# Rows for the feed-forward part: the second pair fetched with the first, and both transposed ahead of the last output projection

## The chip, the cores and the metric

The kernel runs on one core of a Trainium2 chip. It is written in Bass with the Tile framework, which allots buffers from pools, places the semaphore waits and orders each engine's instructions. The engines are TensorE (PE), VectorE (DVE), ScalarE (ACT), GpSimd (POOL) and SyncE (SP, which only issues transfers here). The metric is the device time of one execution in microseconds (us), the median of several runs.

## The reference, cut to what matters

A trunk of two layers over 1024 latent rows and 256 context rows of width 1024. Each layer mixes (attention and a state-space scan side by side, one input and one output projection) and then runs a SwiGLU feed-forward part. The change stands where the one goes over into the other:

```python
for l in range(DEPTH):                       # DEPTH = 2
    update_ctx = l < DEPTH - 1               # the last layer drops the context rows
    h_l = rmsnorm(x_lat, norm_mix_pre[l]) * (1.0 + sc1_l) + sh1_l
    h_c = rmsnorm(x_ctx, norm_mix_pre[l]) * (1.0 + sc1_c) + sh1_c
    m_l, m_c = hybrid_mixer(h_l, h_c, ..., w_out[l], update_ctx)
    x_lat = x_lat + g1_l * rmsnorm(m_l, norm_mix_post[l])

    f_l = rmsnorm(x_lat, norm_ffn_pre[l]) * (1.0 + sc2_l) + sh2_l
    x_lat = x_lat + g2_l * rmsnorm(swiglu(f_l, w_gate[l], w_up[l], w_down[l]), norm_ffn_post[l])
    if update_ctx:
        x_ctx = x_ctx + g1_c * rmsnorm(m_c, norm_mix_post[l])
        f_c = rmsnorm(x_ctx, norm_ffn_pre[l]) * (1.0 + sc2_c) + sh2_c
        x_ctx = x_ctx + g2_c * rmsnorm(swiglu(f_c, ...), norm_ffn_post[l])
```

## The kernel before, in words

**Tiles.** The 1280 rows are ten tiles of 128 rows: tiles 0 and 1 are the context, 2 to 9 the latent rows. Layer 1 takes only tiles 2 to 9 past its attention. Every product in f32 is made of three matmuls on parts: each operand is split into a high part and the rest, and `mm3` (L228 to L230) adds high by high, high by rest and rest by high.

**Weights.** They stream through the kernel in a planned sequence. A 512 KB piece is fetched by SP into one of two buffers `raw_t` (beside the context's feed-forward in layer 0 also into a spare `raw_u`); ACT casts the high part into a slot `w_t` (L114), and DVE or POOL subtracts it from the raw piece for the rest (L115). There are five slots; a slot is free once its matmuls are done, and a raw buffer once both steps have read it.

**Buffers.** `x()` gives one of six buffers `xt` (128 x 1024, a whole row tile), `s2()` one of eight buffers `s2t` (128 x 512). The matmuls write into five PSUM banks `ps_w` and three `ps_s`.

**Attention's end.** Attention works in units of a tile and a group of heads. When a tile's units are done, `oproj` projects it with w_out (L228 to L230, out of `att_wo` or `w_t` and the attention's output `xt` or `att_b`), `postnorm` normalises and gates the result (two DVE steps L832 and one L838) and writes the row tile to memory, where the feed-forward part finds it. The call `early(0)` comes just ahead of the last unit's values, then follows the second-last tile's projection, then `early(1)`, then the last tile's projection (which goes through the weight pieces one by one and frees their slots), then `early(2)`.

**Rows for the feed-forward part.** They are taken in pairs of tiles. `pre_load` fetches a pair into two `xt` buffers (L992), `row_halves` (L380) fetches a tile into two `s2t` buffers of half a row each. `pre_scale` squares and sums each row on ACT (L243, two steps a tile), makes the reciprocal root on POOL (L245, L235, L236) and scales the rows on POOL (L375, one step for a whole tile, two for halves). The flip (`flip_steps`) then makes columns of the pair: sixteen transposes on PE (L402) into four `ps_w` banks, eight scale-and-shift steps on ACT (L405) into four `s2t` buffers, four copies for the high part on POOL (L409) and four subtractions for the rest on DVE (L410), into `hc` (context) or `ha` (latent). With `keep`, the shifted columns also go out to memory (L412), to be combined later. For the pairs of tiles 6, 7 and 8, 9 there are `quads` instead, which transpose (L1016), shift (L1020) and combine the columns with those kept (L1026 to L1034 on DVE and POOL) into the blocks `h_hb`, `h_t3`, `h_t4` that the latent feed-forward multiplies.

**What runs where, before.** `early(0)` fetches and scales the first pair (tiles 0, 1 in layer 0; 2, 3 in layer 1) and, in layer 1, fetches tiles 6, 7 as halves. `early(1)` flips the first pair and fetches and scales the second (tiles 2, 3; in layer 1 tiles 4, 5, and it scales the halves of 6, 7). `early(2)` flips the second pair and in layer 0 fetches and scales the third (tiles 4, 5). After attention, layer 0 runs the context's gate and up projections (L228 to L230, `ps_w<-hc,w_t`), with `fill_c` between their pieces: its first step flips the third pair, later ones run the quads. Layer 1 goes straight to the latent feed-forward, which begins with the quads of tiles 6, 7.

Of the kernel before, what the change touches and what calls it, by code (L numbers as in the profile page):

```python
# [17 lines left out]
P = 128  # L18
# [36 lines left out]
class Trunk:  # L55
# [314 lines left out]
    def pre_scale(self, xs):  # L370
        for a in xs:
            whole = not isinstance(a, list)
            r = self.row_rstd([a[:, 0:512], a[:, 512:1024]] if whole else a, D)
            for b in [a] if whole else a:
                self.nc.gpsimd.tensor_scalar(b, b, r, 1.0, op0=ALU.mult, op1=ALU.mult)  # L375

    def row_halves(self, t, src):
        a = [self.s2(), self.s2()]
        for i in range(2):
            self.nc.sync.dma_start(a[i], self.x_src(src, t)[:, i * 512:(i + 1) * 512])  # L380
        return a
# [5 lines left out]
    def flip_steps(self, xs, span, i, l, which, keep=None):  # L387
        nc = self.nc
        ps = self.psw
        cc = self.cols[l, which]  # L390
        n = len(xs) * P
        nm, v, col0 = span[0], 1 if span[0] == "hc" else 0, 2 * i * P
        if i == 0:
            self.hT[nm] = self.hT_alloc(nm)
        dst = self.hT[nm]
        for k2 in range(0, KT, 2):
            t = ps()
            h = self.s2()
            for k in range(2):
                kt = k2 + k  # L400
                for j, a in enumerate(xs):
                    nc.tensor.transpose(t[:, k * n + j * P:k * n + (j + 1) * P], a[:, kt * P:(kt + 1) * P], self.ident)  # L402
            for k in range(2):
                kt = k2 + k
                nc.scalar.activation(h[:, k * n:(k + 1) * n], t[:, k * n:(k + 1) * n], AF.Identity,  # L405
                                     bias=cc[:, 8 * v + kt:8 * v + kt + 1], scale=cc[:, 16 + 8 * v + kt:17 + 8 * v + kt])
            hv = h[:, 0:2 * n].rearrange("p (k n) -> p k n", k=2)
            hi = dst[:, k2:k2 + 2, 0, col0:col0 + n]
            nc.gpsimd.tensor_scalar(hi, hv, 1.0, 1.0, op0=ALU.mult, op1=ALU.mult)  # L409
            nc.vector.tensor_tensor(dst[:, k2:k2 + 2, 1, col0:col0 + n], hv, hi.bitcast(F32), op=ALU.subtract)  # L410
            if keep:
                nc.scalar.dma_start(keep[k2 // 2, i], h)  # L412
            yield
# [587 lines left out]
    def quads(self, l, xs, i, B):  # L1001
        nc = self.nc
        cc = self.cols[l, 1]
        tt = nc.vector.tensor_tensor
        v = lambda a: a.rearrange("p (k n) -> p k n", k=2)
        for k2 in range(0, 4, 2):
            qa, qb = self.x(), self.x()
            for half in range(2):
                nc.sync.dma_start(qa[:, half * 512:(half + 1) * 512], self.hf_d[l][(k2 + 4 * half) // 2, i])
            for half in range(2):  # L1010
                t = self.psw()
                for k in range(2):
                    kt = k2 + 4 * half + k
                    for j, a in enumerate(xs):
                        rows = a[half][:, kt % 4 * P:(kt % 4 + 1) * P] if isinstance(a, list) else a[:, kt * P:(kt + 1) * P]
                        nc.tensor.transpose(t[:, k * 256 + j * P:k * 256 + (j + 1) * P], rows, self.ident)  # L1016
                for k in range(2):
                    kt = k2 + 4 * half + k
                    o = half * 512 + k * 256
                    nc.scalar.activation(qb[:, o:o + 256], t[:, k * 256:(k + 1) * 256], AF.Identity, bias=cc[:, kt:kt + 1], scale=cc[:, 16 + kt:17 + kt])  # L1020
            b11, b21, b12, b22 = qa[:, 0:512], qa[:, 512:1024], qb[:, 0:512], qb[:, 512:1024]

            def put(name, src, eng):
                d = B[name][:, k2:k2 + 2, :, 256 * i:256 * i + 256]
                nc.scalar.copy(d[:, :, 0], v(src))
                eng.tensor_tensor(d[:, :, 1], v(src), d[:, :, 0].bitcast(F32), op=ALU.subtract)  # L1026

            if l:
                put("B22", b22, nc.vector)
            else:  # L1030
                keep = self.s2()
                nc.gpsimd.tensor_scalar(keep, b22, 1.0, 1.0, op0=ALU.mult, op1=ALU.mult)
                nc.scalar.dma_start(self.b22_d[k2 // 2, i], keep)
            tt(b11, b12, b11, op=ALU.subtract)  # L1034
            tt(b12, b22, b12, op=ALU.subtract)
            tt(b22, b22, b11, op=ALU.subtract)
            put("T2", b22, nc.vector)
            put("T3", b12, nc.vector)
            put("T1", b11, nc.vector)
            tt(b21, b22, b21, op=ALU.subtract)  # L1040
            put("T4", b21, nc.gpsimd)
            yield
# [193 lines left out]
def emit(nc, tc, I, out, dump=None):  # L1236
    with ExitStack() as es:
        k = Trunk(nc, tc, es, I, out)
        k.hT, k.fgrow = {}, (None, None)
        k.plan()  # L1240
        SC, SA, SB = k.SPANS
# [15 lines left out]
        for l in range(DEPTH):  # L1257
# [3 lines left out]
            with tc.tile_pool(name=f"kv{l}", bufs=1, reuse_waits="tile") as kv:  # L1261
# [10 lines left out]
                fl = {}  # L1272

                def early(stage):
                    keep = k.hf_d[l]
                    if stage == 0:
                        cols()
                        fl[0] = k.pre_pair(SC if l == 0 else SA, 0, 2 * l, l, 1, keep if l else None)
                        if l:
                            fl[2] = [k.row_halves(t, 2) for t in (6, 7)]  # L1280
                    elif stage == 1:
                        fl[0]()
                        fl[1] = k.pre_pair(SA, l, 2 * l, l, 1, keep)
                        if l:
                            k.pre_scale(fl[2])
                    else:
                        fl[1]()
                        if l == 0:
                            fl[2] = k.pre_pair(SA, 1, 0, 0, 1, keep)

                gate, ss = k.ssd(l, kv)
                zf = itertools.chain([step(ss)] * (len(qt) - 1), [lambda: None])
# [3 lines left out]
                def zfill():  # L1296
                    i = next(nz)
                    if i == 2:
                        k.att_keys(l)
                    if i == len(qt) - 4:  # L1300
                        k.att_open(l)
                    if i == len(qt) - 2:
                        att.append(k.attention(l, early))
                        next(att[0])
                    next(zf)()
# [95 lines left out]
```

## Time and profile before

| | us |
|---|---|
| median of the runs | 3217.45 |
| lowest and highest of three runs | 3215.97 and 3223.33 |
| the profiled execution | 3221.04 |
| its span, first to last instruction | 3219.3 |
| PE busy | 3034.8 (94%) |
| DVE busy | 1679.0 (52%) |
| POOL busy | 1668.3 (52%) |
| ACT busy | 1410.2 (44%) |
| the 16 DMA engines, mean rate | 159 GB/s |

The mean granted clock of PE was 0.973. Attention of layer 0 ends at about 841 us of the span, with its last projection from 844 to 855 and the context's gate and up projections behind it; attention of layer 1 ends at about 2492 us. In rows of a timeline the columns are the start in us, the us from the first start to the last end, the engine, the line, the operation, what it writes and reads, its shape and count, and in brackets the idle time before it with what ended it; "SPq" is the time that SP's queue waited until it could issue a transfer. In rows of the view by stretches the columns are the stretch, its length, the busy us of PE, of its weight loads, of DVE, ACT and POOL (with counts), the mean granted clock, the DMA share (the mean busy share of the 16 DMA engines) and GB/s.

### The profile page before, as it was taken

The page shows a single profiled execution, that of the slowest core. Times are in us where ns is not written, and L with a number is a line of the kernel's source. Part 1 is how long each engine was busy: PE and PEld are TensorE (multiplying, and loading weights), DVE is VectorE, ACT ScalarE, POOL GpSimd, SP SyncE. Part 2 cuts the span into 40 slices and gives each one's busy share as a digit, 9 for nine tenths or more (in the row PEclk, how much of TensorE's full clock was granted, in tenths as well). Part 3 has the DMA queues.
Part 4 walks back from the last instruction along what each step waited for, and adds up shares of the span by engine and source line. Part 5 has one row for each costly group of instructions (what it writes and reads, how often), then busy time and mean ns, then how long its engine had stood idle before and what let it go on. Part 6 is the DMA issues. An engine that isn't in the chain of part 4 may idle for free.

```text
span 3219.3 us, 45016 instructions
## 1 busy us (share of the span) xinstructions
PE 3034.8 (94%) x16147; PEld 2511.3 (78%) x16147; DVE 1679.0 (52%) x3093; ACT 1410.2 (44%) x2595; POOL 1668.3 (52%) x1529
## 2 busy tenths in 40 slices
PE   6899898999889999999998998899999899999997
PEld 4677687888789777778876777688888688888885
DVE  2556557666575555543021166768665766554003
ACT  4433336666664333332243344337666633333232
POOL 4326556544565444444476634755444555554663
PEclk8899899999999999999998999999999899999999
DMA  6276554222576545547566525653222443336776
GB/s 230 70 218 211 191 164 128 79 66 66 167 226 214 182 149 177 177 151 248 176 234 219 155 61 159 224 177 100 66 66 85 132 133 116 112 112 208 238 247 208
DMA packets 372703, 510.66 MB, mean 159 GB/s; under 512 B 25400, under 2 KB 258520, under 8 KB 372224
## 3 DMA queue, kind: packets, MB, share of 16 engines
q1 hardware_dynamic: 292912, 385.09, 38.4%
q10 hardware_dynamic: 79568, 122.69, 10.4%
q8 instruction: 128, 2.10, 0.3%
q14 instruction: 95, 0.78, 0.1%
HBM read 384.71 MB, written 122.99 MB: 158 GB/s over the span
## 4 chain that ended last, share of the span: by engine, by line
PE 51%; DMA 6%; POOL 4%; DVE 4%; ACT 2%; issue 2%; ACTq 0%; SPq 0%; DVEq 0%; POOLq 0%
PE ps_w L228 9%; PE ps_w L229 9%; PE ps_w L230 9%; PE ps_s L228 5%; PE ps_s L229 5%; PE ps_s L230 5%; DMA raw_t<-in_w_down 3%; POOL w_t L115 2%; PE ps_w L916 2%; PE ps_w L909 2%; PE ps_s L887 2%; ACT w_t L114 1%; PE ps_w L279 1%; DMA raw_t<-in_w_up 0%; PE ps_w L759 0%
## 5 line engine op out<-in xcount | busy, mean ns | idle before, releaser
L115 POOL TENSOR_TENSOR w_t<-raw_t,w_t 128x512 fp32r<-128x512 f32 (+2 forms) x430 | 797.4, 1865 | 812.2 <-ACT w_t L114 766.1
L114 ACT CAST w_t<-raw_t 128x512 fp32r<-128x512 f32 (+2 forms) x470 | 368.2, 799 | 715.2 <-PE ps_s L230 249.0
L888 DVE TENSOR_SCALAR_CACHE_REDUCE att_a<-ps_s 128x512 f32<-128x512 f32 (+1 forms) x400 | 227.0, 586 | 137.2 <-PE ps_s L887 128.3
L896 POOL TENSOR_SCALAR att_a<-att_a,att_st 128x1280 f32<-128x1280 f32 (+1 forms) x144 | 183.1, 1274 | 152.0 <-DVE att_st L895 82.7
L229 PE MATMUL ps_w<-w_t,hid_ring 128*128 128x512 f32 x523 | 207.1, 396 | 8.7 <-POOL w_t L115 8.7
L230 PE MATMUL ps_w<-w_t,hid_ring 128*128 128x512 f32 x523 | 205.7, 394 | 0.0
L894 ACT ACTIVATE att_a<-att_a,att_st 128x1280 f32<-128x1280 f32 (+1 forms) x144 | 183.2, 1273 | 34.5 <-DVE att_st L893 30.3
L909 PE MATMUL ps_w<-cst_all,att_a 128*128 128x128 f32 x1312 | 197.6, 276 | 0.1
L228 PE MATMUL ps_w<-w_t,hid_ring 128*128 128x512 f32 x523 | 195.6, 395 | 2.0 <-ACT w_t L114 1.4
L115 DVE TENSOR_TENSOR xt<-s2t,xt 128x512 fp32r<-128x512 f32 (+2 forms) x145 | 141.2, 975 | 57.7 <-ACT xt L114 55.5
L489 DVE SCALAR_TENSOR_TENSOR xt<-row,convw,xt 128x512 f32<-128x512 f32 (+1 forms) x128 | 125.3, 1032 | 83.9 <-ACT xt L487 64.4
L909 PEld LDWEIGHTS ps_w<-cst_all,att_a 128*128 128x128 f32 x1312 | 153.2, 141 | 11.3 <-DVE xt L832 5.5
L832 DVE SCALAR_TENSOR_TENSOR xt<-ps_w,rstd_t,gate_row 128x512 f32<-128x512 f32 x57 | 40.0, 745 | 232.3 <-POOL rstd_t L236 169.4
L114 ACT CAST xt<-s2t 128x512 fp32r<-128x512 f32 (+2 forms) x145 | 78.7, 543 | 152.5 <-DVE s2t L1145 63.3
L228 PE MATMUL ps_w<-ha,w_t 128*128 128x512 f32 x352 | 138.4, 394 | 2.3 <-ACT xt L1020 2.3
L229 PE MATMUL ps_w<-ha,w_t 128*128 128x512 f32 x352 | 138.5, 393 | 1.9 <-DVE ha L410 1.9
L230 PE MATMUL ps_w<-ha,w_t 128*128 128x512 f32 x352 | 138.0, 392 | 0.0
L229 PEld LDWEIGHTS ps_w<-w_t,hid_ring 128*128 128x128 f32 x523 | 98.7, 189 | 34.2 <-POOL w_t L115 12.1
L228 PEld LDWEIGHTS ps_w<-w_t,hid_ring 128*128 128x128 f32 x523 | 98.5, 189 | 25.3 <-ACT w_t L114 2.7
L115 DVE TENSOR_TENSOR w_t<-raw_t,w_t 128x1024 fp32r<-128x1024 f32 (+1 forms) x40 | 44.2, 1116 | 141.2 <-ACT w_t L114 141.2
L887 PE MATMUL ps_s<-att_c,raw_q 128*128 128x512 f32 (+1 forms) x400 | 109.3, 372 | 7.2 <-DMA raw_q<-q 6.8
L230 PEld LDWEIGHTS ps_w<-w_t,hid_ring 128*128 128x128 f32 x523 | 98.7, 189 | 21.5
(366 smaller groups left out, 8797.7 us busy)
## 6 DMA issues: line engine op xcount, KB each, us to landing
raw_t<-in_w_down SPq DMA_DIRECT2D x132, 512.0 KB
hid<-xt ACTq DMA_DIRECT2D x88, 512.0 KB
raw_t<-in_w_gate SPq DMA_DIRECT2D x70, 512.0 KB
hid_ring<-hid SPq DMA_DIRECT2D x85, 384.0 KB
xt<-in_w_mod SPq DMA_DIRECT2D x56, 512.0 KB
raw_t<-in_w_up SPq DMA_DIRECT2D x46, 512.0 KB
xt<-xs SPq DMA_DIRECT2D x36, 512.0 KB
raw_t<-in_w_in SPq DMA_DIRECT2D x32, 512.0 KB
```

Of the source, the lines that this page charges most:

```text
L114: self.nc.scalar.copy(hi, src)
L115: (eng or self.nc.vector).tensor_tensor(lo, src, hi.bitcast(F32), op=ALU.subtract)
L228: mm(out, st[0], mv[0], start=first, stop=False)
L229: mm(out, st[0], mv[1], start=False, stop=False)
L230: mm(out, st[1], mv[0], start=False, stop=last)
L489: nc.vector.scalar_tensor_tensor(acc, row[:, o0 + k:o0 + k + n], cw[:, ct, k:k + 1], acc, op0=ALU.mult, op1=ALU.add)
L887: nc.tensor.matmul(s[:, :m], qs[t][c][:, hd], kst[:, g, j:j + m], start=c == 0, stop=c == 1)
L888: nc.vector.tensor_scalar(pb[:, j:j + m], s[:, :m], -0.125, None, op0=ALU.mult, op1=ALU.min, accum_out=st[:, n:n + 1])
L894: nc.scalar.activation(pb, pb, AF.Exp, bias=nmx, scale=-1.0, accum_out=st[:, 4:5])
L896: nc.gpsimd.tensor_scalar(pb, pb, st[:, 5:6], 1.0, op0=ALU.mult, op1=ALU.mult)
L909: nc.tensor.transpose(tp[:, (2 * k + h) * P:(2 * k + h + 1) * P], pr[h][:, (k2 + k) * P:(k2 + k + 1) * P], self.ident)
L916: nc.tensor.matmul(av, vst[:, kt, g], pt[:, c, k * 256:(k + 1) * 256], start=kt == 0 and c == 0, stop=kt == nk - 1 and c == 1)
```

## The change

`early(0)` now also fetches the second pair, as halves in four `s2t` buffers, and scales it. `early(1)` flips the first pair, then fetches the third (in layer 0 tiles 4, 5, fetched and scaled; in layer 1 tiles 6, 7, now as whole rows in two `xt` buffers, and scaled), and then flips the second pair. So both flips stand ahead of the last projection, and `early(2)` does nothing. A small function `cols_of` lets the transposes of the flip and of the quads read from halves or from whole rows.

```diff
+    def cols_of(self, a, kt):
+        return a[kt // 4][:, kt % 4 * P:(kt % 4 + 1) * P] if isinstance(a, list) else a[:, kt * P:(kt + 1) * P]
+
...
                 for j, a in enumerate(xs):
-                    nc.tensor.transpose(t[:, k * n + j * P:k * n + (j + 1) * P], a[:, kt * P:(kt + 1) * P], self.ident)
+                    nc.tensor.transpose(t[:, k * n + j * P:k * n + (j + 1) * P], self.cols_of(a, kt), self.ident)
...
                     for j, a in enumerate(xs):
-                        rows = a[half][:, kt % 4 * P:(kt % 4 + 1) * P] if isinstance(a, list) else a[:, kt * P:(kt + 1) * P]
-                        nc.tensor.transpose(t[:, k * 256 + j * P:k * 256 + (j + 1) * P], rows, self.ident)
+                        nc.tensor.transpose(t[:, k * 256 + j * P:k * 256 + (j + 1) * P], self.cols_of(a, kt), self.ident)
...
                     if stage == 0:
                         cols()
                         fl[0] = k.pre_pair(SC if l == 0 else SA, 0, 2 * l, l, 1, keep if l else None)
-                        if l:
-                            fl[2] = [k.row_halves(t, 2) for t in (6, 7)]
+                        xs = [k.row_halves(t, 2 * l) for t in ((4, 5) if l else (2, 3))]
+                        fl[1] = lambda: k.pre_flip(xs, SA, l, l, 1, keep)
+                        k.pre_scale(xs)
                     elif stage == 1:
                         fl[0]()
-                        fl[1] = k.pre_pair(SA, l, 2 * l, l, 1, keep)
                         if l:
+                            fl[2] = k.pre_load(SB, 0, 2)
                             k.pre_scale(fl[2])
-                    else:
+                        else:
+                            fl[2] = k.pre_pair(SA, 1, 0, 0, 1, keep)
                         fl[1]()
-                        if l == 0:
-                            fl[2] = k.pre_pair(SA, 1, 0, 0, 1, keep)
```

The change moves the lines behind it by three (L402 becomes L405, L410 becomes L413, L832 becomes L835) or two (L1016 becomes L1018).

PE around the last projection of layer 0, before: the end of the second-last projection, the first flip, the last projection (out of `w_t` and `att_b`, its rest left out), the second flip, and the context's gate and up projections.

```order
L230 MATMUL ps_w<-att_wo,xt 128x512
L402 MATMUL ps_w<-cst_all,xt 128x128 x16
L228 MATMUL ps_w<-w_t,att_b 128x512
...
L230 MATMUL ps_w<-att_wo,xt 128x512
L402 MATMUL ps_w<-cst_all,xt 128x128 x16
L228 MATMUL ps_w<-hc,w_t 128x256
```

The same place now:

```order
L230 MATMUL ps_w<-att_wo,xt 128x512
L405 MATMUL ps_w<-cst_all,xt 128x128 x16
L405 MATMUL ps_w<-cst_all,s2t 128x128 x16
L228 MATMUL ps_w<-w_t,att_b 128x512
...
L230 MATMUL ps_w<-att_wo,xt 128x512
L228 MATMUL ps_w<-hc,w_t 128x256
```

The second sixteen transposes moved from behind the last projection to ahead of it, and now read half rows (`s2t`).

DVE at the same place, before: the last steps of the second-last tile's normalisation (L832), the first flip's subtractions (into `hc`), three pieces of weights (L115), the last tile's normalisation (L832, L838), and among it the second flip's subtractions (into `ha`).

```order
L410 TENSOR_TENSOR hc<-s2t,hc 128x2x256 x4
L115 TENSOR_TENSOR w_t<-raw_t,w_t 128x1024 x3
L832 SCALAR_TENSOR_TENSOR xt<-ps_w,rstd_t,gate_row 128x512 x2
L410 TENSOR_TENSOR ha<-s2t,ha 128x2x256 x2
L838 TENSOR_TENSOR xt<-xt 128x1024
```

Now:

```order
L413 TENSOR_TENSOR hc<-s2t,hc 128x2x256 x4
L413 TENSOR_TENSOR ha<-s2t,ha 128x2x256 x4
L115 TENSOR_TENSOR w_t<-raw_t,w_t 128x1024 x3
L835 SCALAR_TENSOR_TENSOR xt<-ps_w,rstd_t,gate_row 128x512 x2
L1080 TENSOR_TENSOR s2t<-s2t,ps_w 128x256
```

Four subtractions moved ahead of the three pieces of weights, and the first product of the context's feed-forward (L1080) follows the normalisation's first steps.

PE in layer 1, before: the end of the last projection, thirteen transposes of the second flip (three of its sixteen stand within the projection), the first quads' transposes (L1016), and the latent feed-forward (`ha,w_t`).

```order
L230 MATMUL ps_w<-att_wo,xt 128x512
L402 MATMUL ps_w<-cst_all,xt 128x128 x13
L1016 MATMUL ps_w<-cst_all,s2t 128x128 x16
L228 MATMUL ps_w<-ha,w_t 128x512
```

Now:

```order
L230 MATMUL ps_w<-att_wo,xt 128x512
L1018 MATMUL ps_w<-cst_all,xt 128x128 x16
L228 MATMUL ps_w<-ha,w_t 128x512
```

The second flip is gone from this place (it stands ahead of the last projection, as in layer 0), and the quads read whole rows (`xt`) where they read halves.

## The prediction

> **What bounds the kernel now.** I read the page first, then the busy time by stretches around the two places that the change touches, then TensorE's (PE's) own timeline there, then the queues that end its waits.
>
> ```profile
> span 3219.3 us, 45016 instructions
> PE 3034.8 (94%) x16147; PEld 2511.3 (78%) x16147; DVE 1679.0 (52%) x3093; ACT 1410.2 (44%) x2595; POOL 1668.3 (52%) x1529
> ```
>
> PE is busy for 94% of the span; only its idle time, or time at a low clock, can be won. The view by stretches (busy us of PE, PEld, DVE, ACT, POOL, then the granted clock, the DMA share and GB/s) shows where that is near the change:
>
> ```profile
> 841.00:884.00 43.00, 31.55 (x173) 27.83 (x172) 23.04 (x20) 25.82 (x53) 28.39 (x35) 0.84 0.76 245
> 884.00:920.00 36.00, 36.00 (x303) 35.91 (x302) 24.90 (x28) 24.61 (x48) 24.14 (x22) 1.00 0.78 246
> 864.00:880.00 16.00, 9.90 (x58) 9.70 (x58) 9.24 (x7) 7.02 (x14) 9.30 (x11) 0.71 1.04 342
> 1100.00:1300.00 200.00, 200.00 (x992) 148.88 (x991) 106.91 (x147) 63.83 (x111) 90.01 (x68) 1.00 0.52 174
> 2492.00:2524.00 32.00, 22.19 (x99) 17.04 (x97) 16.12 (x20) 21.80 (x55) 23.21 (x36) 0.81 0.66 214
> 2524.00:2564.00 40.00, 35.75 (x151) 29.12 (x151) 38.05 (x51) 29.79 (x56) 17.11 (x14) 0.89 0.29 92
> ```
>
> The two ends of attention (841 to 884 in layer 0, 2492 to 2524 in layer 1) lose 11.45 and 9.81 us of PE to idleness, and run at 0.84 and 0.81 of the clock. What follows each is full: 1100 to 1300 has PE at 200.00 of 200.00, so time won ahead of it stays won. Two rows warn: at 864 to 880 the DMA share is 1.04, and from 2524 to 2564 VectorE (DVE) is busy 38.05 of 40.
>
> PE's timeline in layer 0 (start, us, what, and in brackets the idle time before it and what ended it):
>
> ```profile
> 841.25 1.47 PE L402 MATMUL ps_w<-cst_all,xt 128*128 128x128 f32 x12
> 844.22 0.50 PE L228 MATMUL ps_w<-w_t,att_b 128*128 128x512 f32 x1 [0.41 <-DVE xt L832]
> 855.32 0.49 PE L402 MATMUL ps_w<-cst_all,xt 128*128 128x128 f32 x3
> 860.73 1.12 PE L402 MATMUL ps_w<-cst_all,xt 128*128 128x128 f32 x4 [3.44 <-ACT s2t L405]
> 861.64 0.58 PE L228 MATMUL ps_w<-hc,w_t 128*128 128x256 f32 x1
> 866.71 0.36 PE L230 MATMUL ps_w<-hc,w_t 128*128 128x256 f32 x1
> 866.90 0.28 PE L228 MATMUL ps_w<-hc,w_t 128*128 128x256 f32 x1
> 869.64 0.28 PE L230 MATMUL ps_w<-hc,w_t 128*128 128x256 f32 x1
> 876.02 1.11 PE L402 MATMUL ps_w<-cst_all,xt 128*128 128x128 f32 x4 [6.10 <-POOL xt L375]
> 883.64 0.39 PE L228 MATMUL ps_w<-hc,w_t 128*128 128x256 f32 x1 [0.79 <-ACT s2t L405]
> ```
>
> The last output projection runs 844.22 to 855.32. The second flip comes behind it and waits 3.44 us for ScalarE (ACT); the third waits 6.10 us for its rows to be scaled. After the 3.44 us wait 24 matmuls take 861.64 to 866.71 (23 steps of 0.22 us), the next 24 take 866.90 to 869.64 (23 steps of 0.119).
>
> The causes lie on the queues:
>
> ```profile
> 824.57 17.21 SPq L992 DMA_DIRECT2D xt<-xs  x2
> 860.93 1.41 SPq L992 DMA_DIRECT2D xt<-xs  x2
> 859.66 1.47 ACT L405 ACTIVATE s2t<-ps_w,cols 128x256 f32<-128x256 f32 x3
> 855.59 1.05 ACT L114 CAST w_t<-raw_t 128x1024 fp32r<-128x1024 f32 x1 [4.19 <-DMA raw_t<-in_w_gate]
> ```
>
> The second pair's second load is issued 17 us behind its first, because it needs an xt buffer; the third pair's loads go out only at 860.93. The second flip's scaling starts at 859.66, behind a weight cast that itself waited 4.19 us for its DMA.
>
> **The change, part by part.** *Layer 0, second pair.* Its loads go to four s2 buffers ahead of the last attention unit; its squares (4 on ACT) and scales (4 half rows on POOL) go there too. That work is hidden by idle time of the two engines:
>
> ```profile
> 834.58 0.75 ACT L920 COPY s2t<-ps_w 64x256 f32<-64x256 f32 x2 [5.07 <-PE ps_w L916]
> 835.41 0.98 POOL L923 TENSOR_TENSOR s2t<-s2t 64x128 f32<-64x128 f32 x2 [6.50 <-ACT s2t L920]
> 886.45 0.68 ACT L243 ACTIVATE junk<-s2t 128x512 f32<-128x512 f32 x1
> 893.89 1.37 POOL L375 TENSOR_SCALAR s2t<-s2t,rstd_t 128x512 f32<-128x512 f32 x2
> ```
>
> Four squares at 0.68 are 2.7 us against 5.07 idle; two tiles' scales at 1.37 are 2.7 us, about 5 with their rstd steps, against 6.50. Were that cover gone they would delay the last projection's input by those 5 us at most. PE has the same 16 transposes, 12 in 1.47 us, so 1.8 us, now between 844.22 and 846.0: the last projection starts 1.8 us later and ends at about 857.1 instead of 855.32. From there the pending second flip is gone, so the context matmuls start at 857.1, not 861.64: 4.5 us won.
>
> *Layer 0, third pair.* Its loads, squares and scales now stand ahead of the last projection, so the rows are ready (about 857) before its transposes. The 6.10 us wait goes, and so do the 0.79 and the slow clock: 24 matmuls at 0.22 instead of 0.119 cost 2.3 us, and the 17 or so behind the second wait about 1.6. Sum: 4.5 + 6.1 + 0.8 + 3.9 = 15.3. Less new waits: the four extra splits on DVE stand ahead of the weight splits, so the next raw loads go out about 3 us later; I take 2.3 us of them as seen by PE. Layer 0: **13.0**. Bounds: 15.3 if nothing waits; 5 if the DMA, at 1.04 from 864 to 880, sets the pace until the third flip is through and only the first 4.5 us stay.
>
> *Layer 1.* The same for its two pairs, with the third pair now whole rows in xt buffers:
>
> ```profile
> 2485.44 0.75 ACT L920 COPY s2t<-ps_w 64x256 f32<-64x256 f32 x2 [5.04 <-PE ps_w L916]
> 2504.72 0.55 PE L402 MATMUL ps_w<-cst_all,xt 128*128 128x128 f32 x3 [3.86 <-POOL xt L375]
> 2516.64 1.11 PE L402 MATMUL ps_w<-cst_all,xt 128*128 128x128 f32 x4 [3.27 <-DVE xt L832]
> 2520.04 1.12 PE L1016 MATMUL ps_w<-cst_all,s2t 128*128 128x128 f32 x4 [1.43 <-ACT xt L1020]
> 2526.15 0.80 PE L229 MATMUL ps_w<-ha,w_t 128*128 128x512 f32 x1 [1.91 <-DVE ha L410]
> 2526.74 0.63 PE L230 MATMUL ps_w<-ha,w_t 128*128 128x512 f32 x1
> 2528.45 0.63 PE L228 MATMUL ps_w<-ha,w_t 128*128 128x512 f32 x1
> 2542.59 0.64 PE L228 MATMUL ps_w<-ha,w_t 128*128 128x512 f32 x1 [2.34 <-ACT xt L1020]
> 2565.71 0.50 PE L229 MATMUL ps_w<-h_hb,w_t 128*128 128x512 f32 x1 [1.19 <-DVE h_hb L1026]
> 2522.66 1.09 DVE L1034 TENSOR_TENSOR xt<-xt 128x512 f32<-128x512 f32 x1
> 2525.41 0.68 DVE L410 TENSOR_TENSOR ha<-s2t,ha 128x512 fp32r<-128x512 f32 x1
> ```
>
> By PE: 3.86 (a wait in the midst of the last projection), 1.43 and 1.91 go; of the 3.27 for a bank that the last normalisation holds, I keep 1.7, since the 16 transposes still stand right behind the projection; the low clock (matmuls 0.43 apart from 2526.74 to 2528.45, 0.23 at full clock) gives about 2.5. That is 3.9 + 1.4 + 1.9 + 1.6 + 2.5 = 11.3. By DVE, which is full until 2564: its chain starts at 2522.66 with L1034, and would start about 8.5 us earlier, since the copies it needs follow the transposes; and the four splits L410 of 0.68 (2.7 us) leave this stretch. That is 11.2. Both say **11**. Bounds: 5 (only the 3.86 and the 1.43 go, and the halves come late) and 15 (PE's row of 2565.71 and the 2.34 go as well).
>
> *The clock, weighed.* A 2.34 us wait ahead of 2542.59 stands for what is left; small waits of that size stay, and the stretch's 0.89 says that they may keep part of the slow clock. I therefore took the low-clock terms only behind waits that go. The Trainium skill (TensorE: Matmul & The Clock Gate, Part 1: The HAM clock gate) says that the clock falls to half after an idle window of about 3.4 us and returns after a busy one; the 3.44 and 6.10 us waits agree, and by it the remaining waits would cost no clock, which would add 1 to 2 us to the gain.
>
> *Sum.* 13 + 11 = 24 us. The profiled execution took 3221.04 us, 1.74 more than its span, and stands 3.6 above the median of 3217.45. The gain is taken off both: span 3195, execution 3197, **median 3193.5**.
>
> **Rivals.** (1) *Transfers and DVE take half of it.* For: the share of 1.04 and DVE's 38.05 of 40. Against: at 884 to 920 PE ran 36.00 of 36.00 with a share of 0.78, so the weight stream can feed it. Then layer 0 keeps 6 and layer 1 6: 3205.5. (2) *Nothing measurable.* The third pair of layer 0 and the quads of layer 1 wait elsewhere, for buffers: the s2 loads of layer 1 already wait for buffers, as the row below shows, and only the 4.5 us of layer 0 stay, less 2: 3215. (3) *Slower.* DVE's queue: the second pair's four splits stand ahead of the weight splits that free the raw buffers, and beside POOL's adding of rows they are slow:
>
> ```profile
> 844.75 3.50 DVE L410 TENSOR_TENSOR hc<-s2t,hc 128x512 fp32r<-128x512 f32 x2
> 2465.06 7.54 SPq L380 DMA_DIRECT2D s2t<-xs  x4
> ```
>
> Two took 3.50 us there, 1.75 each against 0.68 alone. Four at 1.75 put the weight transfers back by 7 us in each layer; if the transfers and not PE set the pace from there on, nothing is won and up to 14 us are lost, 10 as a middle: 3227. It decides from the point at which PE finds weights missing at the start of both feed-forward parts; against it speaks that PE is full at 884 to 920. The Trainium skill (SBUF — State Buffer, Who interferes with whom) has DVE, with two operands in SBUF, and POOL exclude each other there for a whole instruction; the 1.75 agrees with it.
>
> **How the numbers follow.** About 0.2%, 6.4 us, is what a measurement of this kernel tells from no change. Forecast (17 to 31 us won, 3186 to 3200): 0.50; more than that: 0.06; rival 1 (6.5 to 17 won): 0.25; rival 2: 0.12; rival 3: 0.07. So faster 0.81, same 0.12, slower 0.07. The forecast's own range is 3186 to 3200; to hold 8 in 10 it reaches through rival 1 to the edge of rival 2: 3186 to 3212.
>
> **What will show it.** Right: 16 more transposes straight behind the first 16 in both layers with no wait over 1 us, the last projection 1.8 us later and unbroken in layer 1; the wait for L375 of 6.10 gone; the clock at 1.00 in the 4 us behind; the first context unit starting some 16 us behind the end of the second-last projection, where it was 20. Wrong: a cast of weights on ACT that waits for its DMA with PE idle behind it (rival 1 or 3); PE waiting for h_hb or h_t for over 4 us in layer 1 (DVE bounds it); squares on ACT that wait for the half rows, which would hold up the last attention unit.

## The result: 21.5 us faster, 2.6 us above the predicted time

The changed kernel takes 3196.06 us (median of 12 runs, 3185.34 to 3205.24), the kernel before 3217.60 us (12 runs beside it). The ratio is 0.9936 with a 95% interval of 0.9920 to 0.9953, which is 15 to 26 us. The prediction was 3193.5 us and 24 us; its range of 3186 to 3212 holds the result.

The profiled execution took 3199.29 us with a span of 3197.5 us. Its page begins:

```profile
span 3197.5 us, 45009 instructions
PE 3028.3 (95%) x16147; PEld 2507.3 (78%) x16147; DVE 1685.2 (53%) x3093; ACT 1409.8 (44%) x2595; POOL 1674.6 (52%) x1531
```

To see where the time went, the two traces are cut into five stretches: in each layer the one from the first transposes of the first flip to the first matmul of the down projection (the first that reads `hid_ring`), and what lies around these two. These are the rows of PE's timeline in the changed kernel:

```profile
837.78 1.47 PE L405 MATMUL ps_w<-cst_all,xt 128*128 128x128 f32 x12
...
1489.31 0.40 PE L228 MATMUL ps_w<-w_t,hid_ring 128*128 128x512 f32 x1
...
2477.01 1.47 PE L405 MATMUL ps_w<-cst_all,xt 128*128 128x128 f32 x12
...
2946.62 0.39 PE L228 MATMUL ps_w<-w_t,hid_ring 128*128 128x512 f32 x1
```

In the kernel before, the same four matmuls start at 841.25, 1503.28, 2492.17 and 2969.89.

| stretch, us | before | after | won |
|---|---|---|---|
| up to layer 0's first flip (nothing changed there) | 841.3 | 837.8 | 3.5 |
| layer 0, flip to down projection | 662.0 | 651.5 | 10.5 |
| between the two | 988.9 | 987.7 | 1.2 |
| layer 1, flip to down projection | 477.7 | 469.6 | 8.1 |
| from there to the end | 249.4 | 250.9 | -1.5 |

The two stretches that the change touches win 18.6 us (13 and 11 were predicted); the rest is the spread between executions. That spread is large: over the fourteen profiles of this study the first flip of layer 0 stands anywhere between 820.80 and 841.25 us, though next to nothing differs ahead of it. The two stretches that the change touches repeat within 1.7 us in kernels with the same code there, with one exception of 2.8 us (layer 1 of scale_first and tail_and_first), so they tell the kernels below apart better than the medians do.

### The profile page after: what moved, and what is told of

It is laid out like the page before. It is cut to its first block, busy times and chain, and to the rows that moved or that the text cites. A ratio compares the mean times of both kernels' runs of the same rounds, so it can differ in the third digit from the quotient of the medians.

```text
span 3197.5 us, 45009 instructions
## 1 busy us (share of the span) xinstructions
PE 3028.3 (95%) x16147; PEld 2507.3 (78%) x16147; DVE 1685.2 (53%) x3093; ACT 1409.8 (44%) x2595; POOL 1674.6 (52%) x1531
## 4 chain that ended last, share of the span: by engine, by line
PE 54%; DMA 4%; POOL 4%; DVE 3%; ACT 2%; issue 2%; ACTq 0%; DVEq 0%; SPq 0%; POOLq 0%
PE ps_w L228 9%; PE ps_w L229 9%; PE ps_w L230 9%; PE ps_s L228 6%; PE ps_s L229 6%; PE ps_s L230 6%; DMA raw_t<-in_w_down 2%; PE ps_w L919 2%; PE ps_w L912 2%; POOL w_t L115 2%; PE ps_s L890 2%; PE ps_w L279 1%; ACT w_t L114 1%; PE ps_w L762 0%; POOL rstd_t L236 0%
## 5 line engine op out<-in xcount | busy, mean ns | idle before, releaser
L115 POOL TENSOR_TENSOR w_t<-raw_t,w_t 128x512 fp32r<-128x512 f32 (+2 forms) x430 | 797.7, 1866 | 802.2 <-ACT w_t L114 743.7
L897 ACT ACTIVATE att_a<-att_a,att_st 128x1280 f32<-128x1280 f32 (+1 forms) x144 | 183.2, 1273 | 32.8 <-DVE att_st L896 30.5
L115 DVE TENSOR_TENSOR xt<-s2t,xt 128x512 fp32r<-128x512 f32 (+2 forms) x145 | 140.5, 970 | 52.0 <-ACT xt L114 49.6
L835 DVE SCALAR_TENSOR_TENSOR xt<-ps_w,rstd_t,gate_row 128x512 f32<-128x512 f32 x57 | 40.0, 746 | 233.4 <-POOL rstd_t L236 171.2
L115 DVE TENSOR_TENSOR w_t<-raw_t,w_t 128x1024 fp32r<-128x1024 f32 (+1 forms) x40 | 45.0, 1132 | 130.8 <-ACT w_t L114 130.8
```

Of the source, the lines that this page charges most:

```text
L115: (eng or self.nc.vector).tensor_tensor(lo, src, hi.bitcast(F32), op=ALU.subtract)
L897: nc.scalar.activation(pb, pb, AF.Exp, bias=nmx, scale=-1.0, accum_out=st[:, 4:5])
```

## The profile after

The view by stretches, with the columns as in the prediction:

```profile
820.00:838.00 18.00, 18.00 (x108) 15.73 (x108) 5.36 (x11) 9.17 (x24) 8.02 (x18) 1.00 0.25 89
838.00:880.00 42.00, 38.84 (x278) 35.69 (x277) 30.45 (x28) 29.80 (x58) 32.94 (x31) 1.00 0.79 254
1005.00:1023.00 18.00, 14.88 (x68) 10.59 (x67) 9.94 (x14) 7.62 (x15) 11.49 (x9) 0.91 0.68 231
2477.00:2509.00 32.00, 28.14 (x139) 22.96 (x138) 24.92 (x32) 26.96 (x63) 20.79 (x28) 0.95 0.76 247
2509.00:2549.00 40.00, 34.90 (x151) 28.61 (x150) 28.32 (x39) 21.82 (x41) 23.03 (x13) 0.91 0.23 69
```

Ahead of the flip PE is busy for 18.00 of 18.00, so fetching and scaling the second pair under the last attention unit cost PE no idle time there. From 838 to 880 the clock is 1.00, where it was 0.84. In layer 1 the first flip starts 15 us earlier than before, so 2477 to 2509 is the stretch to set beside 2492 to 2524 of the kernel before: its clock is 0.95, where it was 0.81, and PE is busy for 28.14 of 32 us, where it was for 22.19. Two stretches still lose: 1005 to 1023, which is new, and 2509 to 2549, with 34.90 of 40 us and a clock of 0.91, little better than at the same place before (2524 to 2564: 35.75 and 0.89).

PE's timeline in layer 0:

```profile
840.75 1.97 PE L405 MATMUL ps_w<-cst_all,s2t 128*128 128x128 f32 x16 [0.40 <-DVE xt L835]
842.47 0.48 PE L228 MATMUL ps_w<-w_t,att_b 128*128 128x512 f32 x1
...
853.53 0.28 PE L228 MATMUL ps_w<-hc,w_t 128*128 128x256 f32 x1
...
861.06 0.66 PE L405 MATMUL ps_w<-cst_all,xt 128*128 128x128 f32 x4 [1.18 <-ACT s2t L1079]
862.84 1.31 PE L405 MATMUL ps_w<-cst_all,xt 128*128 128x128 f32 x8 [1.13 <-DVE xt L835]
863.91 0.36 PE L228 MATMUL ps_w<-hc,w_t 128*128 128x256 f32 x1
...
1011.39 0.50 PE L228 MATMUL ps_w<-h_t,w_t 128*128 128x512 f32 x1 [3.12 <-ACT s2t L1079]
...
1012.25 0.63 PE L228 MATMUL ps_w<-h_t,w_t 128*128 128x512 f32 x1
1012.68 0.63 PE L229 MATMUL ps_w<-h_t,w_t 128*128 128x512 f32 x1
```

The context's matmuls start 15.8 us behind the first flip (853.53 - 837.78; 20.4 before). The first matmul behind the third flip comes at 26.1 us, and came at 42.4; but before, 72 of the context's matmuls stood ahead of it, and now 48. For the same work, the context's 73rd matmul, the times are 42.4 and 29.1 us (866.86): 13.3 us won by there. Up to the first matmul of the latent part it is 15.2 us: PE's row and SP's fetch of the first weights for that part, before and then now:

```profile
1018.59 0.40 PE L228 MATMUL ps_w<-ha,w_t 128*128 128x512 f32 x1
1001.11 0.37 SPq L209 DMA_DIRECT2D raw_t<-in_w_gate  x1
```

```profile
999.92 0.40 PE L228 MATMUL ps_w<-ha,w_t 128*128 128x512 f32 x1
986.87 0.37 SPq L209 DMA_DIRECT2D raw_t<-in_w_gate  x1
```

Against the first flip PE is 15.2 us earlier (162.1 us for 177.3), the fetch only 10.8 (149.1 for 159.9): the weights' lead on PE fell from 17.5 to 13.1 us. Then some of the gain goes again, at the start of the latent part: a wait of 3.12 us that the kernel before doesn't have, with matmuls 0.43 apart instead of 0.23 for 3 us behind it. ACT is late there. Its timeline in the last pieces of the context:

```profile
988.74 0.38 ACT L1079 ACTIVATE s2t<-ps_w 128x256 f32<-128x256 f32 x1
989.02 1.04 ACT L114 CAST w_t<-raw_t 128x1024 fp32r<-128x1024 f32 x1
...
992.85 0.52 ACTq L1083 DMA_DIRECT2D hid<-xt  x1
993.49 1.05 ACT L114 CAST w_t<-raw_u 128x1024 fp32r<-128x1024 f32 x1 [2.62 <-DVE xt L115]
994.44 0.38 ACT L1079 ACTIVATE s2t<-ps_w 128x256 f32<-128x256 f32 x1
...
1009.92 1.14 ACT L114 CAST w_t<-raw_t 128x512 fp32r<-128x512 f32 x2 [5.05 <-DMA raw_t<-in_w_gate]
```

One turn for one piece (a SiLU, the gate's activation, two casts of weights, the cast of the hidden rows, and the write of these rows, which waits for DVE's split) takes 5.70 us, 988.74 to 994.44. PE's turn, 48 matmuls, is 5.76 us (57.6 us for ten pieces). From the thirteenth piece on, ACT's SiLU comes some 12 us behind the piece's first matmul, where before it was some 7.5 us; at 0.06 us a piece ACT hardly catches up, and the last SiLU stands behind a cast that waits 5.05 us for late weights.

In layer 1 the quads are where it is lost (PE, then POOL, then DVE):

```profile
2493.71 0.55 PE L1018 MATMUL ps_w<-cst_all,xt 128*128 128x128 f32 x3 [0.77 <-POOL xt L375]
...
2496.00 1.35 PE L1018 MATMUL ps_w<-cst_all,xt 128*128 128x128 f32 x9 [1.74 <-POOL xt L375]
...
2515.87 3.41 PE L1018 MATMUL ps_w<-cst_all,xt 128*128 128x128 f32 x14 [5.10 <-POOL xt L375]
```

```profile
2507.56 4.92 POOL L245 TENSOR_TENSOR ss_t<-ss_t 128x1 f32<-128x1 f32 x1 [8.25 <-ACT junk L243]
...
2513.49 2.32 POOL L375 TENSOR_SCALAR xt<-xt,rstd_t 128x1024 f32<-128x1024 f32 x1
```

```profile
2501.51 0.68 DVE L1036 TENSOR_TENSOR xt<-xt 128x512 f32<-128x512 f32 x1
...
2512.35 0.67 DVE L1120 TENSOR_TENSOR s2t<-s2t,ps_w 128x512 f32<-128x512 f32 x1
```

The second quads wait 5.10 us for tile 9's scaled rows (before, PE waited 2.34 us just behind these transposes, for ACT). They are late because POOL's addition of two numbers per row, 0.19 or 0.20 us in most places, takes 4.92 us, while DVE runs back to back, one instruction each 0.60 us. It ends as DVE reaches L1120.

## The experiments

My theory: the early fetch and the early flip are both needed, the two layers add up, and what is missing of the 24 us is lost at two places: ACT's turn in layer 0 (the 3.12 us wait) and POOL's held-up addition in layer 1 (the 5.10 us). The rivals are with each run. All edits are to the changed kernel unless said otherwise; each run is timed against the kernel before on the same chip. The stretches are those of the table above, from one profile of each run.

| run | ratio to before, 95% interval | layer 0 stretch | layer 1 stretch |
|---|---|---|---|
| before | 1 | 662.0 | 477.7 |
| changed | 0.9936 (0.9920 to 0.9953) | 651.5 | 469.6 |
| changed_again | 0.9933 (0.9908 to 0.9958) | 651.5 | 470.4 |
| layer0_only | 0.9979 (0.9964 to 0.9994) | 651.2 | 477.9 |
| layer1_only | 0.9970 (0.9953 to 0.9987) | 661.9 | 470.3 |
| flip_late | 0.9972 (0.9952 to 0.9992) | 656.0 | 475.5 |
| third_late | 0.9996 (0.9982 to 1.0009) | 656.0 | 478.7 |
| hid_sp | 0.9922 (0.9894 to 0.9950) | 651.0 | 470.6 |
| scale_first | 0.9937 (0.9915 to 0.9959) | 652.8 | 465.5 |
| scale_first_act | 0.9934 (0.9910 to 0.9958) | 651.4 | 468.4 |
| hid_tail | 0.9931 (0.9916 to 0.9945) | 645.5 | 469.9 |
| tail_and_first | 0.9914 (0.9898 to 0.9930) | 647.2 | 468.3 |
| before_tail | 0.9990 (0.9978 to 1.0002) | 663.0 | 478.8 |
| copy_dve_first | 0.9918 (0.9896 to 0.9941) | 645.8 | 470.8 |

### One layer at a time

`early` is the changed one where `l == 0` (or where `l == 1`), and the one of before in the other layer.

> The change in layer 0 alone; layer 1 as before. My theory: the two ends of attention are separate and add up. In the two traces, the stretch from the first flip to the first down-projection matmul of layer 0 went from 662.0 to 651.5 us (10.5 won), and in layer 1 the stretch from the first flip to the down projection from 477.7 to 469.6 us (8.1 won). So this kernel keeps the 10.5: median about 3207, and its layer 1 stretch stays at 478. Rival: the rest of the 21.5 us between the medians (some 3 us) comes from the other order of instructions elsewhere in the program and hangs on one of the layers; then this kernel is at 3203 or below, or at 3210 or above.

> The change in layer 1 alone; layer 0 as before. My theory: 8.1 us won, median about 3209.5, and the layer 0 stretch from the first flip to the first down-projection matmul stays at 662. Rival: the gains don't add (the whole change is worth 21.5), so that this one brings under 4 or over 12 us.

> The changed kernel itself, as the measure for the runs beside it on the same chip. The stretch of layer 0 from the first flip to the first down-projection matmul comes out at 651 to 652 us, that of layer 1 from the first flip to the down projection at 469 to 471, and the waits of 3.1 us for h_t in layer 0 and of 5.1 us ahead of the second quads in layer 1 are there again; median 3194 to 3199.

Medians 3210.81 and 3208.14 against 3219.35: 8.5 and 11.2 us, together 19.8. The medians alone would not decide: 3210.81 stands just past the 3210 of layer0_only's rival, beside a kernel before that took 3219.35, and its interval holds 2 to 12 us won. The stretches do: each goes with its own layer and leaves the other alone (651.2 and 477.9; 661.9 and 470.3). The gains are separate and add up; the rival that they hang together falls. The change on its own repeats (3191.28, a little under the 3194 to 3199 expected, on a chip where the kernel before takes 3212.11; stretches 651.5 and 470.4, waits 3.54 and 5.17).

### The early flip without, and the early fetch without

The first puts the second flip behind the last projection again, the second the fetch of the third pair:

```diff
# flip_late
                             fl[2] = k.pre_pair(SA, 1, 0, 0, 1, keep)
-                        fl[1]()
+                    else:
+                        fl[1]()
# third_late
                         fl[0]()
-                        if l:
+                        fl[1]()
+                    else:
+                        if l:
                             fl[2] = k.pre_load(SB, 0, 2)
                             k.pre_scale(fl[2])
                         else:
                             fl[2] = k.pre_pair(SA, 1, 0, 0, 1, keep)
-                        fl[1]()
```

> Rows fetched and scaled as in the changed kernel, but the second flip is written behind the last projection again; the scheduler puts twelve of its sixteen transposes into the midst of the projection and four behind it. It tells the early fetch from the early flip. Theory of the prediction: in layer 0 the 3.44 us wait for ScalarE and part of the third flip's start come back, 3 to 5 us; in layer 1 about 3 of the 8 us: 3196 + 6 to 8 = 3202 to 3204. Rival: once the rows are there early the place of the flip is worth nothing, since the transposes are pulled into the projection: 3194 to 3198.

> Both flips ahead of the last projection as in the changed kernel, but the third pair (tiles 4, 5 in layer 0; 6, 7 in layer 1) is fetched and scaled only behind the last projection. Theory: the 6.10 us wait of layer 0 for scaled rows comes back with its slow clock (1.6 us), and layer 1's quads wait for a load (about 2 us), squares (2.6) and scaling (2.8): together 6 to 8 in each layer, so 3208 to 3212. Rival: in layer 0 the weight stream, not the rows, sets the pace behind the projection, so that only layer 1 loses: 3202 to 3204.

With the late flip, 4.5 us of layer 0's 10.5 go and 5.9 of layer 1's (469.6 to 475.5, where about 3 were expected). With the late fetch, 4.5 go in layer 0 (6 to 8 expected) and all in layer 1 (478.7). By the medians, 3210.20 and 3218.18 against 3219.35, 9.2 and 1.2 us of the gain are left, less than the expected medians said, and the interval of the second includes no gain at all. PE's waits at the places expected, in layer 1 of the first and in layers 0 and 1 of the second:

```profile
2506.33 1.12 PE L405 MATMUL ps_w<-cst_all,s2t 128*128 128x128 f32 x4 [4.18 <-DVE xt L835]
...
2517.17 0.80 PE L229 MATMUL ps_w<-ha,w_t 128*128 128x512 f32 x1 [2.83 <-DVE ha L413]
```

```profile
862.53 1.11 PE L405 MATMUL ps_w<-cst_all,xt 128*128 128x128 f32 x4 [6.88 <-POOL xt L375]
...
2511.37 1.12 PE L1018 MATMUL ps_w<-cst_all,xt 128*128 128x128 f32 x4 [13.86 <-POOL xt L375]
```

So both parts are needed, and the flip's place is worth more than I had thought: a flip behind the projection waits 4.18 us for a bank that the last normalisation holds, and its splits then hold up the first matmul on them by 2.83. In layer 0 the 6.88 us wait costs only 4.5 us, since the later wait at `h_t` is then 0.32 us instead of 3.12: what PE doesn't lose early it loses late, as the next runs show.

### Layer 0: is it ScalarE's turn that takes some back?

The write of the context's hidden rows is issued by SP's queue instead of ACT's, for all 22 pieces (hid_sp) or for the last twelve (hid_tail; before_tail is the same edit on the kernel before):

```diff
# hid_sp
-            nc.scalar.dma_start(self.hid_d[l][ff, :, :, 0:CTX], hd.bitcast(F32))
+            nc.sync.dma_start(self.hid_d[l][ff, :, :, 0:CTX], hd.bitcast(F32))
# hid_tail, before_tail
+            (nc.sync if ff >= 10 else nc.scalar).dma_start(self.hid_d[l][ff, :, :, 0:CTX], hd.bitcast(F32))
```

> The changed kernel, with the context's hidden rows written out by SyncE's queue and not by ScalarE's. Theory: in layer 0, ScalarE's turn for one piece of the context's gate and up (a SiLU, two weight casts, a cast of the hidden rows, and the wait of 2.4 us for VectorE's split ahead of the write) takes 5.70 us, as long as TensorE's 48 matmuls (48 x 0.119 = 5.71), so that ScalarE never makes up what it fell behind at the start, and the next weights come late: 3.12 us wait at h_t and about 1.6 us of slow clock. Without the wait for the split the turn is some 3 us shorter, ScalarE catches up, and the layer 0 stretch goes from 651.5 to about 647. Rival: the transfers or the buffers of the weights set the pace there: 651 to 652 again; or SyncE's queue, which now waits for the split, delays the weights: over 652.

> The changed kernel; of the context's hidden rows only pieces 10 to 21 are written by SyncE's queue, pieces 0 to 9 by ScalarE's as before, so that SyncE's fetch of rows is not held up. On SyncE and ScalarE nothing else moves. Theory: ScalarE makes up its lag in the last pieces, the weights for the latent part are issued some 4 us earlier against TensorE (the first of them 148 to 149 us behind the first flip now, then 144 to 145), the 3.1 to 3.5 us wait at h_t and its slow clock go: layer 0 stretch from 651.5 to about 647. Rival: buffers or transfers set the pace of the weights; the first of them is issued at 148 again and the stretch stays at 651 to 652.

> The kernel before, with the same writes of pieces 10 to 21 on SyncE's queue. Theory: before the change TensorE doesn't wait at h_t, so this brings nothing, the layer 0 stretch stays at 662 (within 1), and the ratio is 1.000. Rival: the write by ScalarE costs time in any case, and the stretch falls by 4 here too.

With all writes on SP the 3 us wait at `h_t` is gone, but the stretch hardly moves (651.0 for the theory's 647): both sides had a part of it. SP's queue now waits for DVE's splits, and the half rows of tiles 8 and 9 go out at 891.09, 70.3 us behind the first flip; in changed_again it was 883.05, 59.3 us behind. PE waits for them (SP's row, then PE's, of hid_sp):

```profile
891.09 2.15 SPq L383 DMA_DIRECT2D s2t<-xs  x4
```

```profile
900.24 0.47 PE L1018 MATMUL ps_w<-cst_all,s2t 128*128 128x128 f32 x1 [6.59 <-POOL s2t L375]
```

hid_tail leaves the rows' fetches alone, and there the theory holds. ACT's timeline, and SP's first fetch of weights for the latent part:

```profile
975.83 1.05 ACT L114 CAST w_t<-raw_t 128x1024 fp32r<-128x1024 f32 x1 [1.55 <-PE ps_w L230]
```

```profile
980.28 0.56 SPq L209 DMA_DIRECT2D raw_t<-in_w_gate  x1
```

ACT now waits for slots that PE frees, so PE sets the pace. The first fetch for the latent part goes out 142.8 us behind the first flip (980.28 - 837.51), where it was 149.1, and 18.3 us ahead of PE, where it was 13.1; the wait at `h_t` is gone and the stretch falls by 6.0 us to 645.5 (647 expected; two later kernels with the same edit took 647.2 and 645.8). On the kernel before, the same edit brings nothing (663.0, ratio 0.999): there PE is late enough for ACT. So the change used up a lead that the weights had, and the turn of ACT, the same in both kernels, became the limit of layer 0. The intervals about the ratios of hid_tail and of the changed kernel, 0.9931 and 0.9936, are too wide to show the 6 us in the whole time.

### Layer 1: what holds up the scaling of tile 9?

```diff
# scale_first
+            self.pre_scale(xs1)
             for _ in self.quads(l, xs0, 0, B):
                 pass
             head(0)
-            self.pre_scale(xs1)
# scale_first_act, also: tile 9 by ScalarE
-            self.pre_scale(xs1)
+            self.pre_scale(xs1[:1])
+            self.pre_scale_act(xs1[1])
...
+        nc.scalar.activation(r, ss[:, 0:1], AF.Identity, bias=ss[:, 1:2], scale=1.0)
+        nc.scalar.activation(r, r, AF.Ln, scale=1.0 / D)
+        nc.scalar.activation(r, r, AF.Exp, scale=-0.5)
+        nc.scalar.activation(a, a, AF.Identity, scale=r)
# copy_dve_first, also with the edits of hid_tail and scale_first
-            nc.scalar.copy(x1, a)
+            (nc.vector.tensor_copy if l and ff == 0 else nc.scalar.copy)(x1, a)
```

tail_and_first is hid_tail and scale_first in one.

> The changed kernel, with the scaling of tiles 8 and 9 in layer 1 written ahead of the first quads, so that ScalarE's squares of tile 9 end some 2 us earlier. Theory: GpSimd's addition of the two sums (0.19 us elsewhere, 4.92 us here) doesn't get through while VectorE runs back to back on two operands from SBUF, and ends only when VectorE takes one operand from PSUM; so earlier squares bring nothing: the addition only gets longer (about 7 us), the second quads' transposes wait 4 to 6 us again, and the layer 1 stretch stays at 469 to 471. Rival: the squares were late, and the wait shrinks by their 2 us: 467 or below.

> As the run before it, and tile 9's sum, reciprocal root (as exp of minus half the log, without the 1e-6 under the root for this tile) and scaling moved from GpSimd to ScalarE. Theory: without GpSimd's starved addition the rows are ready some 3 us earlier, though ScalarE pays two loads of function tables at 1.3 us; the wait ahead of the second quads falls from 5.1 to about 2 us, and the layer 1 stretch to about 466. Rival: VectorE and ScalarE are the bound there, and what is moved onto ScalarE delays the casts for h_hb and h_t as much: 469 to 472.

> The run before it and the earlier scaling of tiles 8 and 9 in layer 1 (the layer 1 stretch went from 470 to 465.5 with that alone) in one kernel. Theory: the two stand in different layers and add up: stretches 647 and 465.5, median some 9 us below the changed kernel's, 0.990 of the kernel before. Rival: the first brings nothing, then 651.5 and 465.5, 0.9915.

> The run with both (writes of pieces 10 to 21 on SyncE, earlier scaling of tiles 8 and 9), and in layer 1 the copy of the first head's product out of PSUM done by VectorE instead of ScalarE. It stands in VectorE's full stretch, some 31.5 to 32 us behind the first flip, where until now VectorE's first instruction with an operand from PSUM comes at 35.3. Theory: GpSimd's addition for tile 9 gets through when VectorE does not hold two operands in SBUF; it comes at 29 us, and now ends with this copy at about 32 instead of 35.5; the rows are ready some 3 us earlier and the layer 1 stretch goes from 468.3 to about 465.5. Rival: GpSimd is held up by VectorE's work whatever it reads, or by something else: the addition ends at 35 to 36 and the stretch stays at 468 to 470. Layer 0: 645 to 647.5 by both.

The profile of scale_first speaks against the theory: the addition came at 2499.77 and took 2.60 us, not 7, PE's wait fell to 2.43, and the stretch to 465.5. tail_and_first has the same edit in layer 1 and speaks for it: the addition came 1.6 us earlier than in the changed kernel (29.0 us behind the first flip, 30.6 there), took 6.48 us, and ended where it always had, 35.5 us behind the flip, as DVE reached L1120. In scale_first, POOL's row and DVE's two at its end, then the same in tail_and_first:

```profile
2499.77 2.60 POOL L245 TENSOR_TENSOR ss_t<-ss_t 128x1 f32<-128x1 f32 x1 [6.35 <-ACT junk L243]
```

```profile
2501.64 0.68 DVE L1028 TENSOR_TENSOR h_t<-xt,h_t 128x512 fp32r<-128x512 f32 x1
2502.26 0.69 DVE L217 TENSOR_TENSOR s2t<-raw_t 128x512 f32<-128x512 f32 x1
```

```profile
2503.24 6.48 POOL L245 TENSOR_TENSOR ss_t<-ss_t 128x1 f32<-128x1 f32 x1 [6.69 <-ACT junk L243]
```

```profile
2509.58 0.68 DVE L1120 TENSOR_TENSOR s2t<-s2t,ps_w 128x512 f32<-128x512 f32 x1
```

In scale_first DVE's step to L217 is 0.62 us instead of 0.60, and the addition ends there; whether that gap is the reason, no run shows. The last run tests the mechanism itself: it puts an instruction that reads PSUM into DVE's full stretch. POOL's rows, and DVE's:

```profile
2489.14 2.92 POOL L245 TENSOR_TENSOR ss_t<-ss_t 128x1 f32<-128x1 f32 x1 [6.64 <-ACT junk L243]
...
2493.07 3.52 POOL L375 TENSOR_SCALAR xt<-xt,rstd_t 128x1024 f32<-128x1024 f32 x1
```

```profile
2491.92 0.68 DVE L1116 COPY s2t<-ps_w 128x512 f32<-128x512 f32 x1
```

The addition ends at 2492.06, 0.14 us into the copy, 31.8 us behind the flip instead of 35.5. So the addition waits for DVE to read PSUM, as the theory said; of the runs with a long addition, scale_first is the one where it got through without that. The gain isn't shown: the scaling behind it, 1.12 us elsewhere, is held up in its turn (3.52 us, until 1.06 us behind the start of DVE's next instruction on PSUM), PE's wait falls from 4.70 to 2.31 us, but the stretch is 470.8, since PE then waits 1.03 us for POOL's part of `h_t`, and 0.64 and 2.08 us for weights (only 1.01 in tail_and_first):

```profile
2551.98 0.47 PE L228 MATMUL ps_w<-h_hc,w_t 128*128 128x512 f32 x1 [2.08 <-ACT w_t L114]
```

By its stretch the theory's 465.5 was wrong, and 470.8 lies even above the rival's 468 to 470. scale_first_act ended between the two (468.4 for 466 or 469 to 472): the wait ahead of the second quads fell to 0.70 and 2.37 us, and waits of 1.26 and 1.41 us came later. So the 5.10 us are a real wait, but PE's way through the quads of layer 1 has DVE, ACT and the weights close behind POOL; the 465.5 of scale_first stands alone, and I don't claim it as shown.

tail_and_first has the lowest ratio, 0.9914, about what its rival named (0.9915), but not for the rival's reason: layer 0 kept its gain (647.2), and layer 1 came to 468.3 for the 465.5 of both. Its stretches add up to 5.7 to 6.4 us less than those of the changed kernel's two profiles, and to no less than hid_tail's, so that the edit of layer 1 adds nothing that these profiles show. Its interval overlaps with the changed kernel's, so that it beats the change is likely, not proven.

## Why the prediction was right, step by step

- **Second pair of layer 0.** Right. The last projection starts 1.7 us later against the first flip (4.69 behind it, 2.97 before; 1.8 predicted), and the context 4.6 us earlier (4.5 predicted). The cover held: no wait ahead of the flip.
- **Third pair of layer 0.** The sum of 15.3 was right in size: 13.3 us are won up to the context's 73rd matmul, the first behind the third flip in the kernel before, and 15.2 up to the end of the context. The 6.10 and the slow clock went; 1.18 and 1.13 us of waits for PSUM banks were not foreseen.
- **"2.3 us of them as seen by PE".** This is the term that failed in layer 0. What was taken back measured 4.7 us (15.2 to 10.5), and not where I had put it: the weights did go out later against PE, but PE lived on their lead for 150 us and paid at the start of the latent part. hid_tail doesn't pay there and ends 16.5 us ahead of the kernel before. Rival 1 named the transfers and DVE. At the same place behind the flip the DMA share is 0.87 (859 to 880) and was 0.90 (862.5 to 883.5), which decides nothing; but none of PE's waits there ends with a weight. One sign of being wrong did come, a cast on ACT that waits 5.05 us for its DMA with PE idle behind it; in hid_tail, where ACT's turn no longer holds DVE's split of the hidden rows, that wait of PE is gone, so ACT's turn made those weights late.
- **Layer 1 by PE, 11.3.** The 3.86, the 1.43 and the 1.91 went. Two terms were mis-sized. Of the 3.27 I had 1.6 won; waits of 0.77, 1.74 and 0.50 us, now for scaled rows, leave 0.3. And the 2.34 that was to stay became 5.10: 2.8 lost. 11.3 - 1.3 - 2.8 = 7.2, for 8.1 measured; most of the rest is the clock's term, below.
- **Layer 1 by DVE, 11.2.** DVE's chain starts 24.5 us behind the flip (2501.51 - 2477.01), 30.5 before: 6.0 earlier, not 8.5. With the 2.7 of moved splits that makes 8.7, near the 8.1. That the two sums agreed on 11 proved nothing, as both left POOL out.
- **The clock.** In the stretch from the flip on it rose from 0.84 to 1.00 in layer 0, as predicted, and from 0.81 to 0.95 in layer 1. PE's idle time in the whole layer 1 stretch fell by 4.5 us (15.3 to 10.7), so 3.6 of the 8.1 us came from faster matmuls, where 2.5 were predicted. By the rule of the Trainium skill (TensorE: Matmul & The Clock Gate, Part 1: The HAM clock gate) the waits under 3.4 us would cost no clock; the 3.12 us wait did, about 1.6 us, and so did the 2.08 us wait of copy_dve_first. That I left that gain out of the sum was right.
- **The rivals.** The second (nothing measurable) and the third (slower) fell. Of the third's mechanism, splits on DVE that hold back the weights, PE shows no wait for a weight ahead of the latent part; what came late there is what hid_tail gives back, not 14 us.
- **The number.** The medians' 21.5 us are nearer to the 24 than the 18.6 us of the two stretches. In the two profiles the rest of the difference, 3.2 us (3.5 + 1.2 - 1.5), lies where nothing was changed, so that the forecast came within 2.6 us is in part luck.

## What to carry to other kernels

Work that is moved from behind a wait to ahead of it wins what the wait costs at that place, and the win can be read from the waits and the slow clock there; what it keeps is decided later, by the lead of the streams that ran on while TensorE stood. So, for each stream that feeds the part behind, compare the turn of its slowest engine with TensorE's turn: where they are nearly equal (5.70 and 5.76 us here), hardly any lead comes back. And where a short instruction on GpSimd stands on the path, look at what VectorE runs at that time before trusting its duration.

## What the runs showed of the hardware

**GpSimd can be passed over for many VectorE instructions.** An addition on 128x1, 0.19 or 0.20 us in most places, took 4.92 us (three times), 4.93, 5.25, 6.48 and 2.92 us at the same place in seven profiles, while VectorE ran two-operand instructions from SBUF at 0.60 us each, and in each of those it ended within 0.2 us of the start of VectorE's next instruction with an operand in PSUM; copy_dve_first moved that instruction and the end moved with it. In an eighth, scale_first, it took 2.60 us and got through between two instructions from SBUF; why is open. The Trainium skill (SBUF — State Buffer, Who interferes with whom) says that a VectorE instruction with two inputs in SBUF contends with a GpSimd instruction that reads SBUF, and one with at most one doesn't, outside VectorE's two-port modes; these runs agree, and add that a waiting GpSimd instruction need not get its turn between two VectorE instructions.

**The clock can fall after a wait of 2.4 us.** The same place in the second layer's input projection, with the same wait in two executions of the changed kernel (PE's timeline, first the first profile, then changed_again):

```profile
1874.08 0.66 PE L501 MATMUL ps_w<-cst_all,xt 128*128 128x128 f32 x4 [2.40 <-ACT xt L493]
...
1875.41 0.28 PE L228 MATMUL ps_s<-hc,w_t 128*128 128x256 f32 x1
1875.53 0.28 PE L229 MATMUL ps_s<-hc,w_t 128*128 128x256 f32 x1
```

```profile
1863.57 0.66 PE L501 MATMUL ps_w<-cst_all,xt 128*128 128x128 f32 x4 [2.40 <-ACT xt L493]
...
1865.47 0.41 PE L228 MATMUL ps_s<-hc,w_t 128*128 128x256 f32 x1
1865.69 0.41 PE L229 MATMUL ps_s<-hc,w_t 128*128 128x256 f32 x1
```

In the first the matmuls behind the wait are 0.12 apart, in the second 0.21 for some 3 us. Ten of the fourteen profiles wait about 2.4 us at this place: in eight the matmuls are slow behind it, in two they aren't. So a wait of 2.4 us can cost clock in one execution and not in the next. Whether this is why executions of one kernel differ as a whole, no run shows.
